# The MLPs of the last two token blocks as one 2x2 block product with seven products, and the sample tokens moved to block 1

## The chip, the core and the metric

The kernel runs on one core of a Trainium2 chip. The metric is device time in microseconds (us), median of three runs. The engines are named as in the profile: PE is TensorE (matmuls; PEld its weight loads), DVE is VectorE, ACT is ScalarE, POOL is GpSimd, SP is SyncE, which here only issues DMAs.

## The reference, cut to what matters

One decoder layer over 2048 prompt tokens and 32 sample tokens (8 sequences of 4), width 1024, MLP width 4096, all fp32:

```
mod = silu(c) @ ada_w + ada_b ;  sh1, sc1, g1, sh2, sc2, g2 = split(mod, 6)
h    = rmsnorm(x) * (1 + sc1) + sh1
proj = h @ w_in                       # columns for three token mixers
y    = concat(ssd(...), rwkv(...), s5(...))     # scans over the tokens, with states
x    = x + g1 * (y @ w_out)
h2   = rmsnorm(x) * (1 + sc2) + sh2
ff   = square(relu(h2 @ mlp_w1)) @ mlp_w2       # 1024 -> 4096 -> 1024
y_out = rmsnorm(x + g2 * ff) ;  the mixers' states are outputs too
```

## The kernel before

**Tiling.** Features lie on the 128 partitions, tokens on the free axis. The prompt is cut into four blocks of 512 tokens (`NB`, `BT`); the 32 sample tokens ride with block `SB` = 2, which is so 544 columns wide (`W`) and is multiplied as two pieces of 272. A PE product is done in `fp32r`, a rounded fp32, as three matmuls per 128x128 weight tile: high part by high part, high by low, low by high (`gemm`, `gemm2`). ACT rounds a tensor to its high part and DVE or POOL subtracts to get the low part, for weights (`wprep`, `wlow`, 512 columns at a time in a ring `wring` of four) and for activations. For blocks 0 and 1 the low part of a weight is split, 224 columns on DVE and 288 on POOL (`WS.POOL`); for blocks 2 and 3 all 512 columns are on DVE.

**Stages.** `in_proj` for blocks 0 to 3; then, block by block, `out_proj`, the last four output tiles of the block before (`w2_chunk` from `HOLD` = 4 on), `final_gen` of the block before (final norm and output) and `mlp`. `mlp` runs eight chunks: four tiles of `mlp_w1` (24 matmuls each) fill the hidden layer, eight tiles of `mlp_w2` (12 each) take it to the output, where DVE adds it to `xs` (`resid`). The MLP of one 512-token block has 1536 matmuls of 128x512. `norm2_gen` makes the second norm's output between `out_proj` and `mlp`.

**Order.** The program is written out by a planner in Python (`Plan`, `pump`): it keeps rough clocks of the engines, and between groups of four matmuls (`SLOT`) it lets waiting generators write their next instructions. The mixers of all blocks (`ssd_gen`, `rw_gen`, `rw_prep`, `rw_post`, `s5_gen`) are such generators: chains of small PE, DVE, ACT and POOL instructions that are interleaved with the large matmuls of `in_proj` and of the MLPs of blocks 0 and 1. `wait_for` and `until` stop the writing of large matmuls until a flag is set, and let only generators write meanwhile. `out_proj(b)` so waits for the mixers of block b alone (`mix_flags`). Buffers come from a few arenas (`Mem`), PSUM banks from two lists: three for large products, five for the rest. All DMAs are issued on SP's queue in program order. Every instruction is recorded by one helper, so a profile row's line is always L198 and groups differ by tiles and shapes: `arena` is fp32 memory, `arena_r` the rounded one, `bk` a PSUM bank.

## Time and profile before

| | us |
|---|---|
| median of 3 runs | 2868.09 (2866.37 to 2869.43) |
| span of the profiled execution | 2863.7 |
| PE busy | 2739.5 |
| DVE busy | 1967.3 |
| ACT busy | 1142.5 |
| POOL busy | 653.5 |

The span is the time between the first and the last instruction of one profiled execution; a run's time also holds what lies around it, here 4.4 us by the median. Stage borders used below are counted off along the program's order of large matmuls: `in_proj` 29 to 799, `out_proj` of block 0 to 870, MLP of block 0 to 1394, MLP of block 1 from 1469 to 1962, of block 2 from 2033 to 2417, of block 3 from 2477 to 2846.

### The profile page before, as it was taken

The numbers are of one execution on the slowest core, as the hardware profiler recorded it, in microseconds if no ns is written. First come the engines' busy times: TensorE is split into PE (matmuls) and PEld (weight loads), VectorE is DVE, ScalarE is ACT, GpSimd is POOL, SyncE is SP. The second block draws the span as 40 slices with busy tenths as digits, with TensorE's granted clock in tenths as the row PEclk, the third lists the DMA queues.
The fourth block names the chain that finished last, engine by engine and source line by source line (L and its number), as shares of the span: only waits on it lengthen the run. The fifth ranks groups of instructions, "written<-read, shape, count | busy, mean of one in ns | idle before, by whom it ended". The sixth has DMA issues, their size and how long they took to land.

```text
span 2863.7 us, 45369 instructions
## 1 busy us (share of the span) xinstructions
PE 2739.5 (96%) x16651; PEld 2265.7 (79%) x16651; DVE 1967.3 (69%) x4567; ACT 1142.5 (40%) x2153; POOL 653.5 (23%) x829
## 2 busy tenths in 40 slices
PE   7999889999999999999999999999999999999997
PEld 4677778877777777777777777778899999888886
DVE  6988996887997877666676778676653535643434
ACT  4354443454335432233443432334534344433342
POOL 1234432233442233322323343321000000000000
PEclk9999999999999999999999999999999999999999
DMA  8467656446553444433434364334222223232222
GB/s 284 155 213 252 201 163 198 164 155 215 170 191 115 144 125 155 146 115 97 159 129 135 118 188 142 120 118 151 96 89 89 89 89 133 82 126 96 99 93 74
DMA packets 302667, 406.26 MB, mean 142 GB/s; under 512 B 85604, under 2 KB 197348, under 8 KB 302444
## 3 DMA queue, kind: packets, MB, share of 16 engines
q1 hardware_dynamic: 302444, 403.36, 42.8%
q8 instruction: 131, 2.15, 0.3%
q14 instruction: 92, 0.75, 0.1%
HBM read 329.67 MB, written 73.62 MB: 141 GB/s over the span
## 4 chain that ended last, share of the span: by engine, by line
PE 62%; DVE 9%; issue 2%; ACT 1%; DMA 1%; POOL 0%; SPq 0%; DVEq 0%; POOLq 0%; ACTq 0%
PE bk L198 62%; DVE arena L198 7%; DVE arena_r L198 2%; ACT arena L198 1%; ACT arena_r L198 1%; DMA arena<-sph 0%; DMA arena<-spk 0%; POOL arena L198 0%; DMA arena<-in_w_out 0%; POOL arena_r L198 0%; DMA arena<-spl 0%; SPq L198 0%; DVEq L198 0%; DVEq L2724 0%; POOLq L198 0%
## 5 line engine op out<-in xcount | busy, mean ns | idle before, releaser
L198 PE MATMUL bk<-arena_r 128*128 128x512 f32 (+1 forms) x11344 | 2284.7, 358 | 61.7 <-DVE arena_r L198 41.5
L198 PEld LDWEIGHTS bk<-arena_r 128*128 128x128 f32 x11344 | 1843.9, 190 | 397.9 <-DVE arena_r L198 65.4
L198 DVE TENSOR_TENSOR arena_r<-arena,arena_r 128x224 fp32r<-128x224 f32 (+2 forms) x981 | 577.7, 610 | 416.9 <-ACT arena_r L198 410.6
L198 ACT ACTIVATE arena_r<-arena 128x512 fp32r<-128x512 f32 (+1 forms) x976 | 581.5, 627 | 468.4 <-PE bk L198 394.3
L198 POOL TENSOR_TENSOR arena_r<-arena,arena_r 128x288 fp32r<-128x288 f32 (+1 forms) x530 | 510.7, 976 | 1055.2 <-ACT arena_r L198 933.2
L198 ACT ACTIVATE arena<-bk 128x512 f32<-128x512 f32 (+8 forms) x619 | 271.9, 459 | 1008.5 <-PE bk L198 798.3
L198 PE MATMUL bk<-arena 128*128 128x128 f32 (+14 forms) x5139 | 540.3, 290 | 50.9 <-DVE arena L198 37.5
L198 PEld LDWEIGHTS bk<-arena 128*128 128x128 f32 (+6 forms) x5139 | 429.7, 152 | 179.7 <-issue 71.2
L198 DVE TENSOR_TENSOR arena<-arena 128x512 f32<-128x512 f32 (+16 forms) x1286 | 515.2, 411 | 51.1 <-ACT arena L198 16.6
L198 DVE SCALAR_TENSOR_TENSOR arena<-bk,arena 128x512 f32<-128x512 f32 (+1 forms) x368 | 235.4, 644 | 269.7 <-PE bk L198 264.0
L198 ACT ACTIVATE arena<-arena 128x512 f32<-128x512 f32 (+4 forms) x445 | 290.1, 664 | 208.1 <-DVE arena L198 189.7
L198 DVE SCALAR_TENSOR_TENSOR arena<-arena 128x512 f32<-128x512 f32 (+9 forms) x605 | 252.2, 430 | 26.6 <-ACT arena L198 6.7
L198 DVE TENSOR_TENSOR arena<-bk,arena 128x512 f32<-128x512 f32 (+4 forms) x277 | 101.2, 381 | 37.0 <-PE bk L198 31.4
L198 POOL TENSOR_TENSOR arena<-arena 128x512 f32<-128x512 f32 (+1 forms) x56 | 73.6, 1320 | 193.5 <-DVE arena L198 100.2
L198 DVE TENSOR_TENSOR arena<-arena,bk 128x512 f32<-128x512 f32 (+2 forms) x163 | 100.4, 627 | 15.3 <-PE bk L198 12.6
L198 DVE SCALAR_TENSOR_TENSOR arena<-arena,bk 64x64 f32<-64x64 f32 (+3 forms) x278 | 91.4, 355 | 27.4 <-PE bk L198 24.1
L198 DVE TENSOR_SCALAR arena<-arena 128x4 f32<-128x4 f32 (+14 forms) x359 | 95.8, 289 | 13.6 <-ACT arena L198 7.8
L198 POOL COPY arena<-arena 128x3 f32<-128x3 f32 (+6 forms) x222 | 70.0, 327 | 47.3 <-ACT arena L198 29.9
L198 ACT ACTIVATE arena<-bk,arena 128x512 f32<-128x512 f32 (+4 forms) x112 | 57.0, 535 | 17.8 <-PE bk L198 16.6
L198 DVE COPY arena<-bk 64x256 f32<-64x256 f32 (+5 forms) x85 | 43.6, 513 | 4.1 <-PE bk L198 2.6
L198 DVE TENSOR_TENSOR_SCAN arena<-arena 128x256 f32<-128x256 f32 (+2 forms) x40 | 36.1, 902 | 1.3
L198 DVE TENSOR_REDUCE arena<-arena 128x4 f32<-128x256 f32 (+1 forms) x34 | 14.0, 412 | 6.7 <-ACT arena L198 6.4
(14 smaller groups left out, 46.3 us busy)
## 6 DMA issues: line engine op xcount, KB each, us to landing
arena<-in_w SPq DMA_DIRECT2D x256, 512.0 KB
arena<-in_w_in SPq DMA_DIRECT2D x88, 512.0 KB
arena<-in_ada_w SPq DMA_DIRECT2D x24, 1024.0 KB
arena<-in_x SPq DMA_DIRECT2D x64, 256.0 KB
arena<-spk SPq DMA_DIRECT2D x32, 512.0 KB
arena<-in_w_out SPq DMA_DIRECT2D x32, 512.0 KB
spk<-arena SPq DMA_DIRECT2D x40, 256.0 KB
spl<-arena SPq DMA_DIRECT2D x33, 256.0 KB
```

The costliest lines, as they stand in the source:

```text
L198: r = fn(*a, **k)
```

## The change

**Pairing.** Only blocks 0 and 1 run `mlp` as before (`NPLAIN` = 2). Blocks 2 and 3 go through a new function `paired`. It takes the two blocks as the two columns of a 2x2 matrix of blocks, and splits the weights' inner and outer dimension in two, so that h2 @ W is a product of 2x2 block matrices. Seven products of sums and differences give what eight plain ones give (the Strassen-Winograd form). For `mlp_w1` the right-hand sums (B11, T2, B21, T3, T1, T4, B22) are made once by `right_gen`. For `mlp_w2` the hidden layer's seven units are made by `hid_gen`, stored to DRAM (`sp_hid`), read back, and split into high and low parts by `hid_load`. The sums of weight blocks (S1 to S4) are made on POOL as the program runs (`Sums`), and all low parts of weights in `paired` past the two `project` calls are made on POOL too.

**What `paired` writes, in order:** the seven state outputs (they stood at the program's end before); `project(0)`, the output projection of block 2; the last four output tiles of block 1's MLP; `project(1)`, for block 3; three early products with B11 and B21 (`NPRE` = 3), while `right_gen` makes the sums; 16 rounds for `mlp_w1` (seven products of 12 matmuls; five in the first three); 16 half rounds for `mlp_w2` (14 products of 6 matmuls); then `final_gen` for both blocks.

**Around it.** `SB` is 1. `mlp` of block 1 waits in its sixth chunk until the mixers of blocks 2 and 3 are all done, since their arena (`arena_b`) is handed over to `paired` as rounded memory (`arena_t`). The RWKV mixer's sample part is written with fewer, wider instructions. The scratch memory for dynamic DMA is made smaller.

```diff
-SB = 2
+SB = 1
+NPLAIN = 2
+NPRE = 3
@@ mlp
+            if b + 1 == NPLAIN and c == 5:
+                for q in range(NPLAIN, NB):
+                    for fl in mix_flags(q) + [("rwb", q)]:
+                        until(fl)
+                A1[:] = [M1]
...
@@ wlow
+                P.tensor_tensor(sm.shape(lo.r), wsrc.pop(i), sm.shape(hi.f), ALU.subtract)
+                sm.drop(wops[i][2])
@@ class Sums
+        def get(self, name):
+            if name == "S2":
+                self.sum("S1", blk("21"), blk("22"), ALU.add)
+                self.sum("S2", self.shape(t["S1"].f), blk("11"), ALU.subtract)
+            elif name == "S3":
+                self.sum("S3", blk("11"), blk("21"), ALU.subtract)
+            elif name == "S4":
+                self.sum("S4", blk("12"), self.shape(t["S2"].f), ALU.subtract)
...
@@ right_gen, for k in (4, 0, 5, 1, 6, 2, 7, 3)
+                scaled(b_[k], bk, k)
+                if k >= 4:
+                    yield 0
+                    continue
+                yield
+                tt(a[k].f, b_[k].f, a[k].f, ALU.subtract)
+                tt(b_[k].f, b_[k + 4].f, b_[k].f, ALU.subtract)
+                yield from put("B22", b_[k + 4].f, True)
+                tt(b_[k + 4].f, b_[k + 4].f, a[k].f, ALU.subtract)
+                tt(a[k + 4].f, a[k + 4].f, b_[k + 4].f, ALU.subtract)
+                yield from put("T2", b_[k + 4].f, True)
+                yield from put("T3", b_[k].f)
...
@@ for p in range(16)
+            product(bkb, wop(), 0, Units("T2"), True)
+            u2 = mal(n)
+            tt(u2.f, u1.f, bkb, ALU.add)
...
+            product(bkc, wop(), 0, Units("T3"), True)
+            tt(u3.f, u2.f, bkc, ALU.add)
+            product(bkd, wop(), 0, Units("T1"), True)
+            tt(c["22"].f, u3.f, bkd, ALU.add)
+            product(bkc, wop(), 0, Units("T4"), False)
+            tt(c["21"].f, u2.f, bkc, ALU.add)
+            product(bkd, wop(), 0, Units("B22"), False)
+            tt(c["12"].f, u2.f, bkd, ALU.add)
...
@@ for c in range(8), half in range(2), nm in UNITS, e, mp in enumerate(mps)
+                        product(bk, w, 256 * e, un, fresh)
+                        if nm == "11" and c == 0:
+                            act(z.f, bk)
+                        elif nm in ("11", "S2"):
+                            tt(z.f, z.f, bk, ALU.add)
+                        elif nm == "12":
+                            add(x11, g0)
...
```

**Where instructions move.** On PE, late in block 1's MLP. Before, groups of large products (`arena_r 128x512`) and of the mixers' small ones take turns:

```order
L198 MATMUL bk_66<-arena_r 128x512 x12
L198 MATMUL bk_68<-arena 128x128 x2
L198 MATMUL bk_70<-arena 64x64 x4
L198 MATMUL bk_69<-arena 32x2x64 x8
L198 MATMUL bk_67<-arena_r 128x512 x12
L198 MATMUL bk_65<-arena_r 128x512 x4
L198 MATMUL bk_72<-arena 32x2x64 x8
L198 MATMUL bk_65<-arena_r 128x512 x16
```

After, from the last large product that stands ahead of the wait in the sixth chunk (`arena_r 128x272`, since the block now carries the sample tokens) on, 385 small ones of the mixers follow without a large one between them (twelve of them read `arena_r` too, in the SSD mixer), of which these are the first:

```order
L201 MATMUL bk_70<-arena_r 128x272 x24
L201 MATMUL bk_72<-arena,arena_b 128x128 x4
L201 MATMUL bk_74<-arena_b,arena 128x512 x2
L201 MATMUL bk_72<-arena_b 64x64 x8
L201 MATMUL bk_73<-arena,arena_b 128x128 x4
L201 MATMUL bk_75<-arena,arena_b 128x1 x4
L201 MATMUL bk_72<-arena_b 32x2x64 x8
L201 MATMUL bk_75<-arena 128x128
L201 MATMUL bk_73<-arena_b 32x2x64 x8
L201 MATMUL bk_76<-arena_b,arena 128x512 x2
```

The mixers' remainder has moved out of the shade of the large products into one piece of its own; on DVE 257 instructions stand in the same piece.

On DVE, between `project(1)` and the first rounds of `mlp_w1`; `bk_74` is the broadcast norm factor of block 3. There `right_gen` stands in four groups of eight instructions, before the first eviction of a `mlp_w1` round that uses one of its sums (the `bk_71` row):

```order
L201 TENSOR_TENSOR arena<-arena,bk_74 128x512 x2
L201 TENSOR_TENSOR arena<-arena 128x512 x4
L201 TENSOR_TENSOR arena_r<-arena,arena_r 128x512 x2
L201 TENSOR_TENSOR arena<-arena,bk_74 128x512 x2
L201 TENSOR_TENSOR arena<-arena 128x512 x4
L201 TENSOR_TENSOR arena_r<-arena,arena_r 128x512
L201 TENSOR_TENSOR arena<-arena,bk_71 128x512
L201 TENSOR_TENSOR arena_r<-arena,arena_r 128x512
```

These are the last two groups; before, `norm2_gen` stood there with two instructions for each of eight feature tiles.

On POOL, in one half round for `mlp_w2`, where before POOL had nothing to do (its last instruction stood in block 1's stretch):

```order
L201 TENSOR_TENSOR arena<-arena 128x512
L201 TENSOR_TENSOR arena_r<-arena,arena_r 128x512 x3
L201 TENSOR_TENSOR arena<-arena 128x512
L201 TENSOR_TENSOR arena_r<-arena,arena_r 128x512 x2
L201 TENSOR_TENSOR arena<-arena 128x512 x2
L201 TENSOR_TENSOR arena_r<-arena,arena_r 128x512 x2
```

Eleven instructions of 512 columns for each round: seven low parts (`arena_r`) and four sums (`arena`).

## Rows read from the trace of the kernel before

**Rows 1.** The page: span, PE and GB/s in 40 slices

```profile
span 2863.7 us, 45369 instructions
PE 2739.5 (96%) x16651; PEld 2265.7 (79%) x16651; DVE 1967.3 (69%) x4567; ACT 1142.5 (40%) x2153; POOL 653.5 (23%) x829
GB/s 284 155 213 252 201 163 198 164 155 215 170 191 115 144 125 155 146 115 97 159 129 135 118 188 142 120 118 151 96 89 89 89 89 133 82 126 96 99 93 74
```

**Rows 2.** Busy time by stretch: MLPs of blocks 0, 1, 2, 3; the tail

```profile
core 0: us, PE busy (x) PEld busy (x) DVE busy (x) ACT busy (x) POOL busy (x), PEclk, DMA share, GB/s
870.00:1394.00 524.00, 518.15 (x3161) 402.98 (x3160) 373.41 (x888) 204.35 (x388) 162.00 (x181) 1.00 0.42 133
1469.00:1962.00 493.00, 475.69 (x2639) 376.41 (x2640) 364.17 (x812) 190.63 (x347) 165.47 (x180) 0.99 0.43 140
2033.00:2417.00 384.00, 379.45 (x2999) 378.38 (x3000) 194.27 (x455) 156.86 (x311) 0.00 (x0) 0.99 0.28 97
2477.00:2846.00 369.00, 363.04 (x1569) 294.33 (x1567) 167.48 (x278) 144.90 (x244) 0.00 (x0) 0.99 0.27 92
2846.00:2863.70 17.70, 4.02 (x24) 3.65 (x24) 7.02 (x19) 0.07 (x1) 0.00 (x0) 0.60 0.41 150
```

**Rows 3.** Busy time by stretch, inside the MLPs of blocks 3 and 2

```profile
2720.00:2820.00 100.00, 100.00 (x435) 81.26 (x434) 39.58 (x61) 38.96 (x66) 0.00 (x0) 1.00 0.27 94
2200.00:2300.00 100.00, 100.00 (x801) 100.00 (x800) 46.60 (x107) 38.28 (x77) 0.00 (x0) 1.00 0.25 85
```

**Rows 4.** Busy time by stretch: the last wait of block 0's `out_proj`

```profile
853.60:870.50 16.90, 15.20 (x139) 13.38 (x137) 13.86 (x32) 8.27 (x16) 2.98 (x4) 0.80 0.23 71
```

**Rows 5.** Groups by form (count | busy us, mean ns | idle), 2520 to 2820, POOL idle

```profile
L198 DVE TENSOR_TENSOR arena_r<-arena,arena_r 128x512 fp32r<-128x512 f32 x135 | 88.1, 684 | 108.5 <-ACT arena_r L198 108.5
L198 ACT ACTIVATE arena_r<-arena 128x512 fp32r<-128x512 f32 x135 | 78.8, 625 | 103.3 <-PE bk L198 102.5
L198 DVE SCALAR_TENSOR_TENSOR arena<-bk,arena 128x512 f32<-128x512 f32 x56 | 42.0, 750 | 66.9 <-PE bk L198 66.9
```

**Rows 6.** Groups by form, 870 to 1394, POOL at work

```profile
L198 DVE SCALAR_TENSOR_TENSOR arena<-bk,arena 128x512 f32<-128x512 f32 x59 | 44.1, 748 | 44.7 <-PE bk L198 44.1
L198 DVE TENSOR_TENSOR arena_r<-arena,arena_r 128x512 fp32r<-128x512 f32 x45 | 38.2, 852 | 13.9 <-ACT arena_r L198 13.6
...
L198 DVE TENSOR_TENSOR arena<-arena 128x1024 f32<-128x1024 f32 x5 | 7.1, 1418 | 0.2
...
L198 POOL TENSOR_TENSOR arena_r<-arena,arena_r 128x512 fp32r<-128x512 f32 x20 | 23.1, 1174 | 5.8 <-PE bk L198 5.8
```

**Rows 7.** Groups by form, the whole run

```profile
L198 DVE SCALAR_TENSOR_TENSOR arena<-arena 128x512 f32<-128x512 f32 x176 | 146.6, 840 | 9.0 <-ACT arena L198 4.5 <-PE bk L198 0.9 <-POOL arena L198 0.8
...
L198 POOL TENSOR_TENSOR arena<-arena 128x504 f32<-128x504 f32 x16 | 26.1, 1637 | 53.9 <-DVE arena L198 53.3 <-PE bk L198 0.7
```

**Rows 8.** Timeline of DVE (start us, us), the last RWKV chunk

```profile
1956.60 0.58 DVE L198 TENSOR_TENSOR arena<-bk,arena 64x128 f32<-64x128 f32 x2
...
1972.23 1.17 DVE L198 SCALAR_TENSOR_TENSOR arena<-arena,bk 64x64 f32<-64x64 f32 x4 [4.17 <-PE bk L198]
...
1982.85 0.88 DVE L198 TENSOR_TENSOR arena<-arena 128x256 f32<-128x256 f32 x2
```

**Rows 9.** Timeline, start of block 3's MLP

```profile
2482.31 12.17 PE L198 MATMUL bk<-arena_r 128*128 128x512 f32 x41 [4.34 <-ACT arena_r L198]
...
2484.22 0.81 ACT L198 ACTIVATE arena<-arena 128x512 f32<-128x512 f32 x1 [1.44 <-DVE arena L198]
```

**Rows 10.** Timeline, the end

```profile
2844.65 0.75 DVE L198 SCALAR_TENSOR_TENSOR arena<-bk,arena 128x512 f32<-128x512 f32 x1 [1.40 <-PE bk L198]
...
2852.15 5.35 DVE L198 SCALAR_TENSOR_TENSOR arena<-arena,bk 128x512 f32<-128x512 f32 x8 [2.17 <-PE bk L198]
...
2857.92 0.45 SPq L198 DMA_DIRECT2D out_p_conv<-arena  x1
...
2860.80 0.43 SPq L198 DMA_DIRECT2D out_p_rwkv<-arena  x1
```

More of the change, by code (lines that the diff above doesn't have):

```diff
@@ new lines, in tail_ops @@
+    def tail_ops(e, block, shape, names):
+        sm = Sums(e, block, shape)
+        for name in names:
+            wops.append([e + 1, sm, name])
+    if len(wseq) % 2:
+        wseq.append((d["w_out"][0], "pad"))
+    flat = lambda t: t
+    for p_ in range(NPRE):
+        e = len(wseq)
+        wseq.append((d["w1"][2 * p_], "m1"))
+        sm = Sums(e, one_block(e), flat)
+        wops.append([e, sm, "11"])
+        wops.append([e, sm, "12"])
+    if len(wseq) % 2:
+        wseq.append((d["w1"][0], "pad"))
@@ L2532, in layer_kernel @@
     for b in range(NB):
-        rest = in_proj(b, nxt[b])
-        next(rest, None)
+        in_proj(b, nxt[b])
     until(("ada", 11))
     last = None
-    for b in range(NB):
+    for b in range(NPLAIN):
         WS.POOL = 0 if b > 1 else 288
```

514 lines of the change are left out of this document (437 added, 77 removed).

## The prediction

> **What bounds the kernel now.** I read the page first, then busy time by stretch, then the groups by form inside stretches with and without POOL, last the timeline where blocks change. PE is busy 96% of the span, so the span is PE's time plus its waits, 2863.7 - 2739.5 = 124 us [rows 1]. By stretch the picture differs. In the MLPs of blocks 2 and 3 PE is nearly always busy while DVE is at half its time and POOL is idle; there a removed matmul is time won. In the MLPs of blocks 0 and 1 the mixers run in the matmuls' shade, DVE is at 71 and 74%, POOL at a third [rows 2]. Inside block 3's MLP 435 matmuls of 128x512 take 100 us, so one costs 0.230 us, at a granted clock of 1.00; a 272-column one costs 0.125 us (801 in 100 us) [rows 3].
>
> **Part 1, the seven products.** The MLP of two blocks has 2 x 1536 = 3072 matmuls of 128x512; an eighth of them, 384, goes. In the order 6832 such matmuls are 6448 after, and the 4512 of 272 columns stay. 384 x 0.230 = **-88.3 us**, all on the path in the stretch where PE is the only busy engine.
>
> **Part 2, the wait in block 1's MLP.** The mixers' rest, hidden before, stands alone: 385 small PE instructions without a large product. The nearest row is the wait at the end of block 0's `out_proj`, where 73 such instructions take 16.9 us with PE busy 15.2 and DVE 13.9 [rows 4]. By PE's count the piece takes 385/73 x 16.9 = 89 us, of which 80 us is PE work that is due in any order: a loss of 9. By DVE's count (257 against 32 records) it takes 257/32 x 13.9 = 112 us: a loss of 32. What stands against both is the chain: of the last RWKV chunk, state and post-processing alone went from 1956.6 to 1983.7 [rows 8], beside large products. I count from the order some four chunks left; one after the other, with the two state steps (15.6 us up to 1972.2) and as much again for the preparation, and 10 us behind the last, they take 4 x 31 + 10 = 134 us, a loss of 54. Below I take 5: the 9 of PE's count rests on one row, and a gain is excluded, since the PE work itself is due in any order. I take **+20 us**, between the two counts, since the same mixture of engines made rows 4. Queued behind the waiting products on PE is the whole rest of the program.
>
> **Part 3, the sums for `mlp_w1`.** `right_gen` starts when block 3's norm factor is there. From the last residual to the first use of such a factor it took 7.5 us [rows 10]; here some of the early products stand in between on PE, about 4 us more. Then come one ACT step of 0.81 [rows 9], four DVE steps of about 0.7, an ACT rounding of 0.63 [rows 5] and a POOL low part of 1.17 [rows 6]: the first T2 unit at about 17 us. Each further group holds eight DVE instructions, 8 x 0.684 = 5.5 us [rows 5], 6 at POOL's side; the fourth unit is there at 17 + 3 x 5.5 = 33.5 to 35 us. PE's cover is three early rounds, 72 x 0.230 = 16.6 us, and 4 us of small matmuls; T2's product would end at 20.6 + 2.8 = 23.4 and ends at about 35: 12 us, and 2 more for what follows such a wait (41 matmuls in 12.2 us instead of 9.4 [rows 9]). **+14 us**, bounds 8 and 20.
>
> **Part 4, the start of `mlp_w2`.** Twelve x tiles of 256 KB are issued on SP at its first product, ahead of 1 MB of weights and of the hidden unit that the fifth product needs: 4.5 MB at the highest rate that the page shows, 284 GB/s [rows 1], is 16 us. The product comes after 4 x 2.76 = 11 us and needs its operand 2.5 us before for the split. **+6 us**, bounds 0 (the queue is ahead) and 12.
>
> **Part 5, the steady rounds.** One round is 84 matmuls, 19.3 us. POOL has 11 instructions, 11 x 1.17 = 12.9 us [rows 6]. DVE has, for `mlp_w1`, five evictions (0.68 to 0.75), three of 0.84 [rows 7] and four of 0.85: 9.5 us; for `mlp_w2`, 14 evictions of about 0.73 and 3.5 splits of 1.42 [rows 6]: 15.2 us. ACT: eleven or so of 0.63 to 0.8, 8 us. DMA: 2.8 MB a round, 145 GB/s, which many slices of the page exceed [rows 1]. All lie below 19.3, so PE should bound; but stretches with DVE at three quarters and POOL at a third have PE waiting 1.1 and 3.5% [rows 2]. On 602 us that is 6 to 21; the stretch had hardly any before. I take **+8 us**, bounds 0 (PE was at 100% there, so no gain) and 21. The rows show what DVE and POOL do to each other: a DVE subtraction with both inputs in SBUF takes 0.684 us with POOL idle [rows 5] and 0.852 beside POOL, an instruction that reads PSUM 0.750 and 0.748 [rows 5, 6]. The Trainium skill, "SBUF — State Buffer", section "Who interferes with whom", says that a DVE instruction with two SBUF inputs and a GpSimd instruction that reads SBUF exclude each other for the whole instruction, the second waiting until the first ends; the rows agree in kind. By that rule the two engines' shares add up in `paired`, and that is the first rival below.
>
> **Part 6, the end.** Two blocks instead of one run `final_gen` last: eight more instructions (5.35 us for eight [rows 10]) and the second norm's small steps, about 1 us, less the seven state outputs, which go from the end to the start of `paired`: 7 x 0.47 = 3.3 us of issue from 2857.9 to 2861.2 [rows 10]. **+3 us**, bounds 0 and 6. In their new place the outputs stand on SP ahead of block 2's x tiles, 3.3 us, which are first needed after 24 matmuls, 5.5 us: covered.
>
> **Part 7, at nothing.** The sample tokens move with all their matmuls; nothing is added. The RWKV sample part needs some 30 DVE instructions fewer beside the matmuls of `in_proj`, where PE bounds too, and the changed arenas reorder the early stretch: 0, with 10 either way. 60 weight loads go, 112 stores and 56 loads of the hidden units come; SP issues one in some 0.47 us, and a store that waits for DVE holds the next weights for a round at most, which the ring of four raw buffers covers.
>
> **The sum.** -88.3 + 20 + 14 + 6 + 8 + 3 = -37 us on 2863.7: a span of 2826.4. The median of the runs lies 4.4 above the span, so the time is **2831 us**.
>
> **Rivals.** (a) *DVE and POOL exclude each other and bound `paired`.* For `mlp_w2` the low parts and sums read weight blocks with strides. The nearest strided POOL row is 1.637 us for 504 columns [rows 7]. With that, 11 x 1.637 + 3.5 x 1.42 = 23.0 us a half round against 19.3, +58 us over 16; in `mlp_w1`, 11 x 1.25 + 3 x 0.84 + 4 x 0.85 = 19.7, +6. 2831 - 8 + 64 = **2887**, slower than before. It decides from a POOL mean of (19.3 - 5.0)/11 = 1.30 us. For it: the rows of contention; against it: contiguous ones are at 1.17, runs of 128 are longer than the 63 of that row, and four of seven low parts are contiguous. (b) *The mixers' chains run one after the other* at the wait, loss 54 instead of 20: **2865**, no change. For it: rows 8; against: rows 4, with DVE busy 82% of such a wait. (c) *Nearly all waits are hidden*: 5 + 8 + 0 + 0 + 3, **2796**. For it: PE waits only 1% beside block 0's mixers; against it: T2's fourth unit has no cover. (d) That the change doesn't do what it says: the order shows the 384 fewer, so I give it nothing.
>
> **How the numbers follow.** The forecast has 0.65, (a) 0.12, (b) 0.08, (c) 0.15. A measurement of this kernel can tell about 0.2%, 6 us, from no change. Forecast and (c) are faster; (b) is half faster, half the same; of (a) 0.10 is slower and 0.02 the same. Faster 0.84, same 0.06, slower 0.10. All low bounds together give -75 - 10 and 2783, all high ones 2903, neither likely at once; the range reaches to (c) below and towards (a) above, leaving out about one in ten on each side: 2795 to 2880.
>
> **What would show it.** In the profile after: 6448 matmuls of 128x512 at 0.230; a stretch of 90 to 110 us late in block 1's MLP with PE at 75 to 90% and DVE above it; a PE wait of about 12 us before the first products with T2, released by POOL or DVE; PE at 97% or more in the steady rounds, with POOL near 1.2 us an instruction. Wrong would be the forecast if the steady rounds take over 20 us each, or if the wait for the mixers leaves PE idle for half of it.

## The result, and the profile after

The changed kernel takes 2937.5 us (median; 2932.9 to 2945.8) against 2868.8 for the kernel before on the same chip: 1.0242 times as long, interval 1.0221 to 1.0263. The forecast was 2831, with 2795 to 2880 as its range. The profiled execution spans 2931.1 us, 67.4 more than before; the forecast span was 2826.4. So 105 us have to be found.

The page of the changed kernel, span, PE's row and the granted clock in 40 slices, answers to [rows 1]:

```profile
span 2931.1 us, 45771 instructions
...
PE 2703.2 (92%) x16267; PEld 2238.9 (76%) x16267; DVE 2120.2 (72%) x4588; ACT 1100.8 (38%) x2049; POOL 1212.6 (41%) x1220
...
PEclk9999999999999999999999999978998999999998
```

PE's idle time went from 2863.7 - 2739.5 = 124 us to 2931.1 - 2703.2 = 228, so the waits grew by 104. PE's busy time fell by 36, where the 384 matmuls that are gone are worth 88, so 52 are missing. The groups of PE's large forms say where most of them are (count | busy us, mean ns of one | idle); first before, then after:

```profile
L198 PE MATMUL bk<-arena_r 128*128 128x512 f32 x6832 | 1693.3, 401 | 46.7 <-DVE arena_r L198 34.3 <-ACT arena_r L198 10.9 <-POOL arena_r L198 0.7
L198 PE MATMUL bk<-arena_r 128*128 128x272 f32 x4512 | 593.2, 292 | 15.0 <-ACT arena_r L198 7.7 <-DVE arena_r L198 7.2
```

```profile
L201 PE MATMUL bk<-arena_r 128*128 128x512 f32 x4864 | 1230.0, 403 | 58.2 <-DVE arena_r L201 27.2 <-ACT arena_r L201 24.8 <-DVE arena L201 2.2
L201 PE MATMUL bk<-arena_r 128*128 128x272 f32 x4512 | 614.6, 294 | 46.4 <-DVE arena_r L201 22.5 <-ACT arena_r L201 13.1 <-DVE arena L201 8.9
...
L201 PE MATMUL bk<-arena_t,arena_r 128*128 128x512 f32 x1584 | 399.3, 402 | 26.6 <-DVE arena_t L201 12.0 <-ACT arena_t L201 7.7 <-ACT arena L201 3.7
```

4864 + 1584 = 6448 matmuls of 128x512, as the order said. But they took 1230.0 + 399.3 = 1629.3 us, where 1693.3 - 88.3 = 1605.0 were left to do: 24 us more. The 4512 of 272 columns took 21 us more, and the mixers' small ones the rest. There is more waiting, and PE is slower around the waits.

Busy time by stretch of the changed kernel, to be read beside [rows 2] and [rows 3]. In order: MLP of block 1 up to the wait, and the wait; the three early rounds and the first full round of `mlp_w1`; steady rounds of `mlp_w1` (3 to 15); the first half round of `mlp_w2`; later half rounds; from the last large matmul to the end:

```profile
core 0: us, PE busy (x) PEld busy (x) DVE busy (x) ACT busy (x) POOL busy (x), PEclk, DMA share, GB/s
1466.80:1865.60 398.80, 380.62 (x3110) 355.33 (x3110) 319.40 (x810) 147.84 (x305) 120.35 (x130) 0.98 0.40 125
1865.60:1998.30 132.70, 92.62 (x692) 68.81 (x693) 85.42 (x257) 30.27 (x67) 15.13 (x16) 0.75 0.27 85
2219.30:2287.60 68.30, 40.44 (x157) 29.73 (x156) 36.60 (x48) 27.06 (x46) 40.84 (x30) 0.78 0.14 50
2306.00:2550.00 244.00, 242.12 (x1042) 196.51 (x1042) 122.49 (x153) 70.22 (x123) 187.68 (x137) 0.99 0.43 157
2571.00:2609.00 38.00, 26.00 (x84) 18.97 (x83) 24.86 (x25) 13.82 (x18) 18.82 (x13) 0.82 0.78 296
2630.00:2860.00 230.00, 228.97 (x993) 185.74 (x992) 188.35 (x210) 90.42 (x124) 201.91 (x132) 1.00 0.41 142
2905.60:2931.10 25.50, 9.52 (x49) 8.84 (x48) 19.41 (x47) 2.05 (x4) 0.00 (x0) 0.60 0.43 165
```

The steady stretches are as forecast: 1042 matmuls in 244 us and 993 in 230 are 0.234 and 0.232 us each, with PE at 99%. Three stretches stand out by PE's share and clock: the wait in block 1's MLP (70% busy, clock 0.75), the start of `mlp_w1` (59%, 0.78) and the start of `mlp_w2` (68%, 0.82).

**The wait.** The timeline of PE on either side of it (start us, us):

```profile
1858.65 6.87 PE L201 MATMUL bk<-arena_r 128*128 128x272 f32 x52
...
1998.37 11.84 PE L201 MATMUL bk<-arena_r 128*128 128x272 f32 x77
```

In between stand 132.7 us with small PE work only. No engine is full in them: PE 70%, DVE 64%, ACT 23%, POOL 11%. DVE's timeline shows the last state steps of four RWKV chunks, 31, 17 and 28 us apart:

```profile
1896.15 1.22 DVE L201 SCALAR_TENSOR_TENSOR arena<-arena,bk 64x64 f32<-64x64 f32 x4 [0.80 <-PE bk L201]
...
1926.67 1.16 DVE L201 SCALAR_TENSOR_TENSOR arena<-arena,bk 64x64 f32<-64x64 f32 x4 [0.18 <-PE bk L201]
...
1943.46 1.22 DVE L201 SCALAR_TENSOR_TENSOR arena<-arena,bk 64x64 f32<-64x64 f32 x4
...
1971.78 1.22 DVE L201 SCALAR_TENSOR_TENSOR arena<-arena,bk 64x64 f32<-64x64 f32 x4 [1.32 <-PE bk L201]
```

**The start of `mlp_w1`.** PE's timeline in the first full round, where T2's product takes one unit after the other:

```profile
2244.51 0.50 PE L201 MATMUL bk<-arena_t,arena_r 128*128 128x512 f32 x1 [0.71 <-POOL arena_r L201]
2252.72 0.79 PE L201 MATMUL bk<-arena_t,arena_r 128*128 128x512 f32 x1 [7.70 <-ACT arena_t L201]
...
2262.31 0.80 PE L201 MATMUL bk<-arena_r 128*128 128x512 f32 x1 [7.03 <-ACT arena_r L201]
...
2271.91 0.80 PE L201 MATMUL bk<-arena_r 128*128 128x512 f32 x1 [7.02 <-ACT arena_r L201]
```

The units come 9.6 us apart; the prediction had 5.5 to 6. DVE's timeline shows what fills one such step: eight instructions, 8.1 us, and two short waits for ACT, 1.5 us:

```profile
2256.17 1.27 DVE L201 TENSOR_TENSOR arena<-arena,bk 128x512 f32<-128x512 f32 x2
2258.43 3.89 DVE L201 TENSOR_TENSOR arena<-arena 128x512 f32<-128x512 f32 x4 [0.99 <-ACT arena L201]
2262.81 3.02 DVE L201 TENSOR_TENSOR arena_r<-arena,arena_r 128x512 fp32r<-128x512 f32 x2 [0.49 <-ACT arena_r L201]
2265.76 1.27 DVE L201 TENSOR_TENSOR arena<-arena,bk 128x512 f32<-128x512 f32 x2
```

### The profile page after: what moved, and what is told of

Same layout as the page of the kernel before. It is cut to its first block, busy times and chain, and to the rows that moved or that the text cites. A ratio compares the mean times of both kernels' runs of the same rounds, so it can differ in the third digit from the quotient of the medians.

```text
span 2931.1 us, 45771 instructions
## 1 busy us (share of the span) xinstructions
PE 2703.2 (92%) x16267; PEld 2238.9 (76%) x16267; DVE 2120.2 (72%) x4588; ACT 1100.8 (38%) x2049; POOL 1212.6 (41%) x1220
## 4 chain that ended last, share of the span: by engine, by line
PE 55%; DVE 13%; issue 3%; ACT 2%; DMA 2%; SPq 1%; POOL 0%; DVEq 0%; ACTq 0%; POOLq 0%
PE bk L201 55%; DVE arena_b L201 6%; DVE arena L201 5%; DVE arena_r L201 2%; ACT arena_b L201 1%; SPq L201 1%; ACT arena_r L201 1%; DVE arena_t L201 0%; DMA arena_b<-in_st_ssd 0%; ACT arena L201 0%; DMA arena_b<-spx 0%; DMA arena<-in_x 0%; DMA arena<-spr 0%; DMA spl<-arena_b 0%; POOL arena_r L201 0%
## 5 line engine op out<-in xcount | busy, mean ns | idle before, releaser
L201 PE MATMUL bk<-arena_r 128*128 128x512 f32 (+1 forms) x9376 | 1841.2, 351 | 104.7 <-DVE arena_r L201 49.7
L201 PEld LDWEIGHTS bk<-arena_r 128*128 128x128 f32 x9376 | 1495.2, 191 | 360.6 <-DVE arena_r L201 64.8
L201 POOL TENSOR_TENSOR arena_r<-arena,arena_r 128x288 fp32r<-128x288 f32 (+2 forms) x795 | 880.7, 1121 | 1461.8 <-ACT arena_r L201 1282.6
L201 ACT ACTIVATE arena_b<-bk 128x512 f32<-128x512 f32 (+9 forms) x453 | 192.9, 448 | 754.1 <-PE bk L201 513.6
L201 DVE TENSOR_TENSOR arena_r<-arena,arena_r 128x224 fp32r<-128x224 f32 (+2 forms) x552 | 294.8, 542 | 204.4 <-ACT arena_r L201 200.3
L201 PE MATMUL bk<-arena_t,arena_r 128*128 128x512 f32 x1584 | 399.3, 402 | 26.6 <-DVE arena_t L201 12.0
L201 PEld LDWEIGHTS bk<-arena_t,arena_r 128*128 128x128 f32 x1584 | 302.8, 192 | 102.9 <-DVE arena_t L201 14.5
L201 DVE TENSOR_TENSOR arena_b<-arena_b 128x256 f32<-128x256 f32 (+17 forms) x531 | 267.6, 512 | 22.5 <-ACT arena_b L201 8.1
L201 DVE SCALAR_TENSOR_TENSOR arena<-bk,arena 128x512 f32<-128x512 f32 (+2 forms) x330 | 200.9, 627 | 104.4 <-PE bk L201 103.2
L201 PE MATMUL bk<-arena_b 32*32 32x128 f32 (+9 forms) x2352 | 215.8, 278 | 17.7 <-DVE arena_b L201 6.0
```

The lines of the kernel that those rows point to most:

```text
L201: r = fn(*a, **k)
```

## The experiments

Each run stands beside runs of the kernel before on its chip. The last column is the ratio's distance from 1, times 2869; the intervals reach 4 to 7 us to either side, so a difference between two runs is uncertain by 6 to 9 us.

| run | what | us | ratio (interval) | against before |
|---|---|---|---|---|
| | the change | 2937.5 | 1.0242 (1.0221 to 1.0263) | +69 |
| e1 | before, sample tokens in block 1 | 2897.3 | 1.0084 (1.0065 to 1.0103) | +24 |
| e2 | e1 and the wait | 2980.8 | 1.0373 (1.0351 to 1.0396) | +107 |
| e13 | e1 and the wait for block 2 alone | 2894.7 | 1.0087 (1.0064 to 1.0109) | +25 |
| e5 | e1, smaller request for room | 2899.4 | 1.0110 (1.0091 to 1.0130) | +32 |
| e9 | before, no MLP for sample tokens | 2840.1 | 0.9905 (0.9887 to 0.9924) | -27 |
| e10 | e1, no MLP for sample tokens | 2849.8 | 0.9938 (0.9921 to 0.9955) | -18 |
| e3 | change, wait late | 2891.8 | 1.0071 (1.0050 to 1.0092) | +20 |
| e4 | change, six early rounds | 2932.9 | 1.0217 (1.0199 to 1.0234) | +62 |
| e6 | e3, sums in passes | 2892.8 | 1.0085 (1.0068 to 1.0102) | +24 |
| e7 | e3, mixers earlier | 2929.2 | 1.0206 (1.0181 to 1.0232) | +59 |
| e8 | e7 with e6's passes and more | 2930.0 | 1.0215 (1.0198 to 1.0233) | +62 |
| e11 | e3, four generators for the sums | 2887.6 | 1.0074 (1.0059 to 1.0090) | +21 |
| e12 | e11, x tiles earlier | 2890.2 | 1.0075 (1.0052 to 1.0098) | +22 |
| e14 | e11, low parts on DVE | 2878.8 | 1.0030 (1.0015 to 1.0045) | +9 |
| e15 | e14, five early rounds | 2884.7 | 1.0052 (1.0032 to 1.0071) | +15 |
| e16 | e14, hidden units first | 2880.1 | 1.0040 (1.0027 to 1.0053) | +11 |
| e17 | e16, swap behind block 2's `out_proj` | 2886.4 | 1.0064 (1.0045 to 1.0083) | +18 |

### The change taken apart: the move, the wait, the seven products

e1, one line of the kernel before:

```diff
-SB = 2
+SB = 1
```

> The kernel before with one edit: the sample tokens go with block 1 instead of block 2. No wait in block 1's MLP, no arena swap, eight products. In the changed kernel 104 us are missing against the forecast. Theory W (the wait): the price is that of the wait in block 1's MLP, the move alone costs nothing where mixers of blocks 2 and 3 may run on until out_proj of those blocks: 2869, within 8 us either way. Theory M (the move): the sample part of the RWKV stage holds up the mixers of the blocks behind it and lengthens the stages up to block 1's MLP, as the longer out_proj stages of the changed kernel suggest (93 + 72 us instead of 72 + 60): 2895 to 2915 here. Theory S (the seven-product section is what is dear): 2869 as well, so this run tells M from the other two.

e2, the same and, in `mlp`:

```diff
         for c in range(7):
+            if b == 1 and c == 5:
+                for q in range(2, NB):
+                    for fl in mix_flags(q) + [("rwb", q)]:
+                        until(fl)
```

> The kernel before with two edits: sample tokens with block 1, and the wait for all mixers of blocks 2 and 3 in block 1's MLP at chunk 5. Nothing else of the change. Theory W: the mixers left at that place (some 300 small PE instructions, the RWKV chunks one behind the other) take 130 to 150 us nearly alone on PE, of which 80 to 95 is PE work that is due anyway: 45 to 65 us above the run with the sample tokens alone, so 2915 to 2930. Theory M: most is in the move, the wait adds the 20 us of the forecast: 20 above the run with the move alone. Theory S: both small, 2870 to 2890.

Measured: +24 for the move (theory W had none, theory M 25 to 45), and 107 - 24 = +83 for the wait, more than any theory had. What is left of the change, the seven products with all that goes with them, is 69 - 107 = -38. The traces bear it out. In e2 as in the change the mixers are done at the end of block 1's MLP; from there to the end, first e2, then the change:

```profile
2111.80:2970.30 858.50, 832.84 (x3680) 679.11 (x3678) 400.99 (x679) 332.24 (x559) 0.00 (x0) 0.98 0.31 102
```

```profile
2110.30:2931.10 820.80, 759.00 (x3296) 613.46 (x3294) 550.98 (x726) 290.94 (x455) 561.52 (x398) 0.96 0.42 150
```

That is 37.7 us less, with 384 matmuls fewer. The section is a gain, as forecast (without the wait and with the move at nothing the forecast was -57). The wait and the move make it a loss. In e2 the stretch of the wait, by the same view, is longer than in the change and emptier:

```profile
1828.80:1999.60 170.80, 103.26 (x755) 78.13 (x755) 107.59 (x310) 34.45 (x76) 21.43 (x21) 0.70 0.25 72
```

e13, e2 without block 3 in the wait:

```diff
-                        until(fl)
+                        if q == 2:
+                            until(fl)
```

> The kernel before with the sample tokens in block 1 (2897) and a wait at chunk 5 of block 1's MLP for the mixers of block 2 alone, where the run with the wait for blocks 2 and 3 took 2981. Theory: what the wait costs is block 3's mixers, which without a pair of blocks are due only at block 3's out_proj, some 490 us later; block 2's are due 180 us later anyway and nearly done. In the order the largest piece without a large product is 20 small PE instructions here and 174 there. 2897 to 2907. If any wait for all of a block's mixers at that place costs (the mixers stand in the order of their ranks, a chunk of block 2 as late as one of block 3): 2920 or more.

Measured: +25, the same as without any wait (e1, +24). The price is that of block 3's mixers alone: taken singly, block 3's `out_proj` needs them only some 490 us later, and a pair needs its arena now.

e3, the changed kernel with the wait at the other end of block 1's MLP:

```diff
@@ mlp, loop over the chunks
-            if b + 1 == NPLAIN and c == 5:
-                for q in range(NPLAIN, NB):
...
@@ mlp, behind the last w2_chunk
+        if b + 1 == NPLAIN:
+            for q in range(NPLAIN, NB):
...
```

> The changed kernel with the wait moved from chunk 5 of block 1's MLP to behind its last product (the accumulator of the squares then lies in M1, as the residuals do). Some 107 us of products of that MLP then run beside the mixers' rest; in the order the largest piece without a large product falls from 150 small PE instructions to 60. Theory W: 35 to 50 us below the changed kernel, 2890 to 2900. Theory S: the section of seven products bears the loss, so less than 15 us: 2922 to 2937.

Measured: 69 - 20 = 49 us less, theory W. (The expectation counts pieces between any two products of `arena_r`, the SSD mixer's among them; so its largest piece is 150 where the whole wait has 385.) The last stretch of block 1's MLP still shows a wait, 50 us of PE work in 63 at clock 0.88:

```profile
2000.00:2063.40 63.40, 49.96 (x394) 44.18 (x394) 49.86 (x139) 25.76 (x55) 12.88 (x14) 0.88 0.29 92
```

### Why the move costs 24 us

e5, `rw_gen` of the block with the sample tokens asks for less room:

```diff
-        spawn(after([("pre", b)] + prev, rw_gen(b), C_RW + (2600 if b == SB else 0), R_RW(b), ("rwb", b)), R_RW(b))
+        spawn(after([("pre", b)] + prev, rw_gen(b), C_RW, R_RW(b), ("rwb", b)), R_RW(b))
```

> The kernel before with the sample tokens in block 1, as in the run with the move alone (2897, 24 above before), and with one number changed: rw_gen of the block with the sample tokens asks for 7200 columns of the mixers' room at its start instead of 9800. Theory A (admission): the larger request stands at the head of the queue until 9800 columns are free, every mixer behind it starts later, and block 0's MLP hides less of them; in the order block 0's MLP holds 603 small PE instructions with the move alone, 888 before, 708 here. Then about a third of the 24 us and what was pushed into block 2's out_proj (147 small PE instructions there, none here) come back: 2875 to 2886. Theory B (the sample part itself is dear where it now stands, in DVE and PE work): unchanged, 2892 to 2902.

Measured: +32 against +24, the intervals overlap: theory A falls. The mixers moved forward as the order said, and nothing came back: block 0's MLP took 510 us instead of 481, and from the last tiles of block 0's `mlp_w2`, behind block 1's `out_proj`, to the start of block 1's MLP 48 us passed instead of 18, with PE idle for 26 of them.

e9 and e10 leave out the MLP of the sample tokens, once in block 2 and once in block 1:

```diff
-        w1_tail(b, gemm(ap, b == SB, drop), hid)
+        w1_tail(b, gemm(ap, False, drop), hid)
...
@@ w2_chunk, and so in mlp
-        hasS = b == SB
+        hasS = False
```

> The kernel before with the MLP of the 32 sample tokens left out (their columns of the residual go on to the end as they are); block 2's MLP is then 1536 products of 512 columns instead of 3072 of 272. By the rows this takes 1536 x (0.250 - 0.230) = 31 us off a stage where PE is the only busy engine: 2838, within 6. It is the base for the next run.

> The same with the sample tokens in block 1 (the move alone, 24 us above before), their MLP left out. Theory D: the move costs because the sample tokens' part of the MLP, its 272-column products, evictions and splits, now stands in the MLP that DVE shares with the mixers, while in block 2's it had DVE half free; without that part the move is free, so 0 to 8 us above the run before this one, 2838 to 2846. Theory M: the price lies in the sample part of the mixers and of in_proj and out_proj, which comes earlier than before and pushes other mixers back: 24 above, 2862.

Measured: -27 and -18, a price of 9 or 10 for the move without that MLP where it was 24 with it. So the larger part, some 14 us (give or take 9), lies in the MLP of the sample tokens, as theory D has it: 272-column products, with twice the evictions, in an MLP where DVE also has the mixers (74% busy there before, 51% in block 2's [rows 2]). That DVE's load is what makes them dearer there was not tested by itself, and what makes the other 10 was not found.

### The rest of the wait

e7, e3 with e5's edit and

```diff
-    MARGIN2, LAG4 = 1100, 2300
+    MARGIN2, LAG4 = 600, 3500
```

> The changed kernel with the wait late (2892), the sample tokens' rw_gen at 7200 columns, and the planner's two numbers for the mixers beside the MLPs at margin 600 and lag 3500 instead of 1100 and 2300, so that mixers are written earlier in the program. In the order block 0's MLP then holds 786 small PE instructions instead of 629, and the largest piece without a large product in block 1's MLP falls from 60 to 20. Theory A: what is left of the wait and of the move goes, 20 to 30 us: 2862 to 2872. If the order on DVE then makes the large products wait elsewhere in block 0's MLP: 2885 to 2900.

Measured: 39 us slower than e3. Busy time of the MLPs of blocks 0 and 1, first e7, then e3:

```profile
892.97:1443.00 550.03, 521.55 (x2926) 409.10 (x2927) 404.62 (x932) 198.77 (x367) 160.68 (x191) 0.97 0.43 133
...
1553.70:2101.10 547.40, 519.75 (x4287) 487.90 (x4287) 397.04 (x1024) 200.90 (x418) 144.23 (x161) 0.98 0.37 118
```

```profile
885.80:1370.50 484.70, 475.60 (x2684) 375.36 (x2684) 334.42 (x740) 182.62 (x335) 159.96 (x181) 0.99 0.43 136
...
1464.20:2063.40 599.20, 563.46 (x4666) 522.79 (x4667) 464.60 (x1201) 221.17 (x459) 165.39 (x180) 0.97 0.39 122
```

242 more PE records in block 0's MLP cost 65 us there and give back 52 in block 1's. PE's idle time in block 0's MLP goes from 9 to 28 us, and its clock from 0.99 to 0.97. (Block 0's MLP also starts 7 us later, and the stretch between the MLPs takes 17 more.) Mixers that are written earlier are no longer ready when PE comes to them; that this is their chains of DVE and ACT steps was not tested.

e17, e16 (below) with the wait and the swap moved behind `project(0)`:

```diff
@@ mlp, behind the last w2_chunk
-        if b + 1 == NPLAIN:
...
@@ paired
-        spawn(y2_gen(), 0.3)
         project(0, ys, left_gen)
+        for q in blocks:
...
+        wait_for(lambda: MB1.used == 0, "swap")
...
+        spawn(y2_gen(), 0.01)
```

> The run before this one with the wait for block 3's mixers, and the swap of the arena with it, moved once more, from the end of block 1's MLP to behind block 2's out_proj; y2_gen, which splits block 3's y for its out_proj, then starts behind the swap instead of ahead of block 2's out_proj, at the front of the order. With the wait late the last 63 us of block 1's MLP hold PE work of 44 us; that loss of 19 goes behind 44 us of block 2's out_proj. y2_gen's eight loads and splits (46 us in the changed kernel, beside other work) then have only the 15 us of the last chunk of block 1's mlp_w2 as cover: at 2.5 us each 20 us, a loss of 5 to 8. Sum: 11 to 14 less than the run before. If y2_gen takes as long as now: 15 us slower.

Measured: no gain, +18 against +11. Block 1's MLP, block 2's `out_proj`, the last chunk of block 1's `mlp_w2` and block 3's `out_proj` took 570.9, 57.0, 29.6 and 57.4 us; in e16 the same four took 602.6, 46.7, 14.8 and 52.3. The 32 us won in the first come back in the other three: 10, 15 and 5. Ahead of a pair stands a path through block 3's last mixers, their y and `out_proj`, and moving the swap only moves where PE waits for it.

### The start of `mlp_w1`

e4, `NPRE = 6` instead of 3 in the change:

> The changed kernel with six instead of three early rounds (products with block 2's own units alone) ahead of the first product with T2: 72 more matmuls, 16.6 us, stand where PE waited for the sums of right_gen. In the trace that piece (early rounds and first full round) takes 68 us where its 132 matmuls need 30. Forecast from the wait there: 16 us less, 2921. If the sums are late because DVE, ACT and POOL are slow and not because of when they begin, each early round is worth its full 5.5 us: 2921 too. If PE's wait only moves (the units B11 and B21 wait for the same engines), 2932 to 2940.

e6, e3 with `right_gen` in passes:

```diff
+                yield from put("T2", b_[k + 4].f)
...
+            for k in range(4):
+                yield from put("T3", b_[k].f)
...
```

> The changed kernel with the wait late (2892) and right_gen in passes: all four B22 and T2 first, then T3, then T1, then T4, instead of all five operands of a unit at a time; T2's low part goes to DVE instead of POOL. In the changed kernel PE got T2's units 9.6 us apart, three such gaps in the first full round. Per T2 unit the passes leave two scalings, four subtractions and a low part on DVE instead of eight to ten instructions in all: some 5.5 to 6.5 us apart. If DVE's count sets the spacing: 10 us less, 2882. If the chain of ACT and POOL low parts in between sets it (each step waits for another engine), 2888 to 2892. If later operands then come late instead: 2892 or more.

e11, e3 with `right_gen` as four generators:

```diff
-            for k in (4, 0, 5, 1, 6, 2, 7, 3):
+            def one(k):
...
+            for k in range(4):
+                spawn(one(k), 0.001 * k)
```

> The changed kernel with the wait late (2892) and right_gen as four generators, one for each pair of units, instead of one that takes the pairs one after the other; the same instructions. In the trace T2's units came 9.6 us apart while DVE was at 61%, ACT at 41% and POOL at 66% in that stretch, and passes in another order left the time where it was. Theory chain: each step waits for another engine and the one generator lets nothing else be written in between; with four of them PE loses 10 to 15 us less in the first full round, 2877 to 2882. Theory engines: the units' own DVE, ACT and POOL time sets the end, 2888 to 2894. If the first unit comes later because all four share the engines: 2892 or more.

Measured: -7 against the change for e4 (16 expected; the intervals overlap), and +24 and +21 against e3's +20 for e6 and e11, no difference. In e11 T2's units no longer come 9.6 us apart, but the early rounds wait instead: early rounds and first full round together take 59.1 us against 67.0 in e3. The whole does not show these 8 us, nor can it rule them out. So neither another order of the sums, nor four generators, nor more cover takes the loss away by itself. DVE's groups by form in that stretch of the change point to another cause; the number behind the busy time is the mean of one in ns:

```profile
L201 DVE TENSOR_TENSOR arena<-arena 128x512 f32<-128x512 f32 x16 | 16.0, 999 | 6.0 <-ACT arena L201 4.0 <-POOL arena_t L201 1.5
L201 DVE TENSOR_TENSOR arena_r<-arena,arena_r 128x512 fp32r<-128x512 f32 x5 | 7.7, 1554 | 1.0 <-ACT arena_r L201 1.0
L201 DVE TENSOR_TENSOR arena<-arena,bk 128x512 f32<-128x512 f32 x9 | 5.8, 679 | 2.6 <-PE bk L201 2.6
```

and POOL's there:

```profile
L201 POOL TENSOR_TENSOR arena_r<-arena,arena_r 128x512 fp32r<-128x512 f32 x12 | 17.4, 1459 | 13.3 <-ACT arena_r L201 13.3
```

A subtraction with both inputs in SBUF takes 1.00 or 1.55 us instead of 0.684 [rows 5], POOL's 1.46 instead of 1.17 [rows 6], and a DVE instruction that reads PSUM 0.679. (e6 moved T2's four low parts from POOL to DVE, but left eight others there.) e14 takes POOL out of `right_gen`, on e11:

```diff
-                yield from put("T2", k, b_[k + 4].f, True)
+                yield from put("T2", k, b_[k + 4].f)
```

(and so for B22 and T1; `True` puts the low part on POOL).

> The run with four generators for right_gen (2888) with the twelve low parts that it gives to POOL on DVE. In its trace DVE's subtractions with both inputs in SBUF took 1.20 and 1.57 us there instead of the 0.68 they take with POOL idle, and those that read PSUM 0.68. Theory exclusion: the two engines' SBUF work adds up, 24 x 0.68 on DVE and 12 x 1.17 plus the weights' low parts on POOL; twelve at 0.68 instead of 1.17 take 6 us off: 2880 to 2884. If the engines work side by side: DVE's own work grows by 8 us, 2888 to 2896.

Measured: +9 against e11's +21, 12 us less. That is theory exclusion: the 6 us expected lie at the edge of what the intervals leave (6 to 19). DVE has twelve instructions more, and those with two inputs in SBUF are still shorter, means of 0.84 and 1.22 us, in e14:

```profile
L201 DVE TENSOR_TENSOR arena_r<-arena,arena_r 128x512 fp32r<-128x512 f32 x12 | 13.9, 1217 | 0.0
L201 DVE TENSOR_TENSOR arena<-arena 128x512 f32<-128x512 f32 x16 | 13.2, 841 | 0.9 <-ACT arena L201 0.5
```

than in e11:

```profile
L201 DVE TENSOR_TENSOR arena<-arena 128x512 f32<-128x512 f32 x16 | 18.6, 1195 | 3.2 <-POOL arena_t L201 2.4 <-ACT arena L201 0.5
L201 DVE TENSOR_TENSOR arena_r<-arena,arena_r 128x512 fp32r<-128x512 f32 x6 | 9.2, 1570 | 0.0
```

The stretch takes 54.7 us against 59.1. The spans of the two profiled executions differ by 6 us, so 4.4 of 6 lie here; whether the rest of the 12 is more than scatter is open. The weights' low parts are still on POOL.

e15, e14 with `NPRE = 5`:

> The run before with five early rounds instead of three: 48 matmuls, 11 us, in front of the first product with T2. If the early rounds run while right_gen works: 8 to 11 us below the run before, 2872 to 2876. In the run with six of them on the changed kernel only 5 of 16 us came back, with POOL at 63% and DVE at 52% beside them; if the early rounds' own steps (two low parts of weights on POOL, one eviction and one rounding on ACT each) push right_gen back: 0 to 4 us below.

Measured: +15 against +9, no gain; the spans of the two profiled executions are equal, 2878.4 and 2878.6. In e15's trace the first full round runs without a wait, 60 matmuls in 13.8 us, so T2's units are in time. But the early rounds in front of it wait, 10.9 us in all, each time for an ACT instruction that empties a PSUM bank. With more cover the loss moves from T2's product to the early rounds.

### The start of `mlp_w2`

e12, e11 with the first four x tiles loaded from round 12 on:

```diff
             for mp in range(4):
+                if mp:
+                    yield from need("rounds")
...
+            if p == 12:
+                spawn(x_load(), 0.3)
```

e8, e7 with e6's passes, a fourth early round, and half of the x tiles behind the first chunk's hidden units:

```diff
             for mp in range(4):
+                while mp > 1 and len(HU[0]) < 7:
+                    yield
```

e16, e14 with hidden units first, and `final_gen` of each block started inside the last chunk:

```diff
-                spawn(hid_load(), 0.25)
+                spawn(hid_load(), 0.02)
...
+                    spawn(late(0), 0.01)
+                    spawn(late(1), 0.01)
```

> The run before with the first four x tiles and their sum tile (1 MB of the 4 MB that x_load brings at the start of mlp_w2) loaded from round 12 of mlp_w1 on instead of behind round 15. The first half round of mlp_w2 lost 19 us, in a stretch where DMA moved 296 GB/s. If the transfers set that loss: 1 of the 11 MB of that stretch less, 3 to 4 us below the run before. If the split of the hidden units on ACT and DVE sets it, or their memory, which is free only when mlp_w1's units are spent: no difference within 3 us. If the tiles taken early leave too little memory for rounds 12 to 15: slower by 5 or more.

> All together on the changed kernel: wait late, mixers early (both edits of the run before), right_gen in passes, four early rounds instead of three, and x_load stops behind its first eight tiles until the seven hidden units of the first chunk are split, so that these stand ahead of the other eight x tiles on SP. If the parts add up: 2867 - 10 (sums) - 2 (a fourth early round) - 5 (of the 19 us that the first half round of mlp_w2 lost) = 2850, 0.7% below the kernel before. If the mixers' part gives nothing: 2875.

> The run with right_gen as four generators and its low parts on DVE (2879), with two edits. hid_load goes ahead of hid_gen in the planner's order (rank 0.02 instead of 0.25), so that the splits of mlp_w2's first hidden units don't stand on DVE behind round 15's differences, which only the last chunk needs; and final_gen of each block starts as soon as its own norm is there, not behind the loop. If DVE's order sets the 19 us that the first half round of mlp_w2 loses: 8 to 12 us less there, 2868 to 2871. If the transfers set it (16 MB between 2558 and 2598 in the changed kernel, at about 400 GB/s): the half round stays at 38 to 40 us. The end: 2 us less if block 2's outputs run beside the last product, else nothing, since DVE is busy 87% of the last half round and the end.

The first half round took 38.2 us in the change and 39.9 in e11, 40.0 in e12, 43.6 in e8, 39.5 in e14, 34.8 in e16; 84 matmuls are 19.3. A quarter of the x tiles earlier (e12) or half of them later (e8) gave nothing, so it does not hang on where these 1 or 2 MB stand. Ahead on DVE the hidden units gave 5 us, as the first theory of e16 has it, but that is a quarter of the loss, and the whole of e16 shows no gain (+11 against +9). What remains fits the transfers: GB/s of the change in 40 slices of 2550 to 2612 us stands near 400 from 2562 to 2598:

```profile
GB/s 11 0 0 0 166 342 254 285 407 404 366 386 404 410 403 407 418 408 391 407 379 363 375 406 378 382 406 411 412 418 398 284 37 0 0 0 0 0 0 0
```

That was not tested by taking the transfers away.

As for e8 as a whole, it inherits e7's loss: +62 beside e7's +59. No version that does the whole work beat the kernel before; the nearest is e14, +9.

## Why the prediction was wrong, step by step

| part | forecast | found | from |
|---|---|---|---|
| 1, seven products | -88 | -88 | 6448 matmuls, 0.232 to 0.234 us in steady rounds |
| 2, the wait | +20 | +53 | 132.7 us less the 80 of PE work due; e3 takes 49 of it away |
| 3, the sums | +14 | +34 | 68.3 us less 132 x 0.230 and 4 |
| 4, start of `mlp_w2` | +6 | +19 | 38.2 less 19.3 us |
| 5, steady rounds | +8 | +7 | 556 us for 2388 matmuls |
| 6, the end | +3 | +11 | 49.3 us less 19.3, against 19.1 before |
| 7, the sample tokens | 0 | +24 | e1 |

The found parts add up to +60 of the +67 us of the span. That they come so near is partly luck. Parts 3 to 5 are taken against PE's bare time, and eight products do not run at that either: in e2 the MLPs of blocks 2 and 3 take 717.7 us for 3024 matmuls, 22 more than 0.230 each. The forecast made the same slip, which brought it nearer to the result. The section's two stretches in e2 and the change are the cleaner measure: -38, where parts 1 and 3 to 6 as found add up to -17. By that the wait, with what else the change does ahead of the pair, costs 67 + 38 - 24 = 81 us and not 53; e2 gives 83.

Some of the difference lies at the front, which part 7 put at 0 "with 10 either way". From the start to block 0's MLP, first before, then the change, then e1:

```profile
0.00:870.50 870.50, 799.62 (x5077) 636.71 (x5077) 735.45 (x1818) 381.71 (x755) 299.58 (x433) 0.97 0.60 194
```

```profile
0.00:886.00 886.00, 802.47 (x5037) 638.85 (x5037) 687.09 (x1728) 379.30 (x759) 294.33 (x427) 0.96 0.56 184
```

```profile
0.00:845.40 845.40, 783.94 (x4963) 620.10 (x4963) 669.54 (x1670) 376.92 (x755) 290.51 (x419) 0.97 0.59 192
```

PE idles 71 us there before, 84 in the change and 61 in e1, which has the move alone. Whether the new arenas or the rewritten RWKV sample part make it was not tested.

**Part 2** failed where a value was chosen between two counts. Three stood there: 89 us for the piece by PE's count, 112 by DVE's, 134 by the chain of four RWKV chunks. The piece took 132.7. The forecast lay between the first two because [rows 4] were taken for the same mixture of engines. But in [rows 4] DVE was busy 82% of the time, and here 64%: it was not the same mixture, and the chunks came one behind the other, as [rows 8] had shown it. Rival (b) described it; its chance of 0.08 was the error. That the count of 134 comes within 2 us is partly luck: it had four steps of 31 us and 10 behind the last, and the trace has steps of 31, 17 and 28 and 25 behind the last. That the chain sets the piece is read from the trace (no engine full, the state steps 17 to 31 us apart), and no run took the chain away. That the wait as such is the price, and that block 3's mixers are, is shown by e2, e3 and e13.

**Part 7** was put at nothing because "the sample tokens move with all their matmuls". It did not ask beside what they stand afterwards. The rows were there: DVE at 51% in block 2's MLP and at 74% in block 1's [rows 2]. e1 gives 24 us, e9 and e10 some 14 of them for the MLP's part. (e1 has the RWKV sample part as it was; in the changed kernel the move was not taken by itself.)

**Part 3** had the right wait and the wrong spacing: eight DVE instructions of 0.684 for a unit, with POOL beside them for nothing. In the trace the eight take 8.1 us, and 1.5 of waiting for ACT come on top. T2's first unit came at 22.5 us behind the last residual instead of 17, partly because its low part stood on POOL behind sums and a low part of weights, and the fourth at 54 instead of 35. The prediction used the exclusion of DVE and POOL for a rival on the steady rounds, but not here, where DVE and POOL work on the same sums. The Trainium skill, "SBUF — State Buffer", section "Who interferes with whom", says that a DVE instruction with two SBUF inputs contends with a GpSimd instruction that reads SBUF, and that one with at most one SBUF input outside the two-port modes does not; the trace agrees: 1.00 and 1.55 us instead of 0.684, and 0.679 for the ones that read PSUM.

**Rival (a)** put that exclusion into the steady rounds, to decide from a POOL mean of 1.30 us. The mean was above that, first from 2300 to 2560 us (steady rounds of `mlp_w1`), then from 2650 to 2850 (half rounds):

```profile
L201 POOL TENSOR_TENSOR arena_r<-arena,arena_r 128x512 fp32r<-128x512 f32 x93 | 128.8, 1403 | 56.8 <-ACT arena_r L201 56.8
```

```profile
L201 POOL TENSOR_TENSOR arena_r<-arena,arena_r 128x512 fp32r<-128x512 f32 x74 | 115.4, 1576 | 25.2 <-ACT arena_r L201 25.2
```

Yet PE stayed at 99%. A mean of 1.58 already holds POOL's waits for DVE: in the timeline an undisturbed POOL instruction takes 1.3 us, one that meets a DVE split up to 2.3. The rival's sum set its 1.637 as POOL's own time and added DVE's to it. By undisturbed times the two engines need 11 x 1.30 + 3.5 x 1.22 = 18.6 us, just below a half round's 19.3. So the exclusion is there, but it does not bound, by a small margin, and part 5 was right: 1212 matmuls in 283.4 us and 1176 in 272.6 are 4.6 and 2.1 us over 0.230 each.

**Part 4** took 4.5 MB at 284 GB/s, the highest slice of the page. It left out what goes over the same queue there: 14 stores of the last round's hidden units (256 KB each), and 13 loads of hidden units and 4 of weights (512 KB each), with the x tiles some 16 MB. They run from 2557 to 2598, and a first half round without loss would end at 2571 + 19 = 2590. The mechanism may be right and the size was wrong, by a count that left most of the queue out; that transfers set all of it was not shown.

**Part 6** counted the outputs and not what DVE does before them. The timeline of the end, PE's last large matmuls, the last sum of squares, and the outputs on DVE:

```profile
2899.85 5.76 PE L201 MATMUL bk<-arena_t,arena_r 128*128 128x512 f32 x24
...
2909.17 2.31 DVE L201 TENSOR_TENSOR arena<-arena 128x512 f32<-128x512 f32 x3
...
2917.06 10.62 DVE L201 SCALAR_TENSOR_TENSOR arena<-arena,bk 128x512 f32<-128x512 f32 x16
```

The 16 outputs take 10.62 us, 5.3 more than the eight of [rows 10], as forecast. But behind PE's end at 2905.6 DVE needs 5.9 us more for the last evictions, the sums of z and the squares. Before it was 1.4: there the last eviction ended at 2845.4 [rows 10], and PE began the norm at 2846. And the last half round takes 23.8 us instead of 19.3.

**The clock** stands in no part of its own. PE's products ran at down to half speed behind the longer waits (the last section), so such a wait cost more than its idle time: 24 us idle made 30.6 in the first full round (44.4 us instead of 13.8), 12 made 19 in the first half round of `mlp_w2`. Part 3 had 2 us for that.

## What to carry to other kernels

When a change has two blocks of work start together, find what the second one needs, and price its whole remaining path by its chain too: here, where no engine was full, the longest count came out and not one in the middle. Moved work can cost by what it stands beside afterwards, even if not one instruction is added. Moving a wait later helps as long as other work can run in front of it (e3, 49 us), and stops helping where the next consumer needs the same result (e17). Before sums are shared out between DVE and POOL, count the instructions with two inputs in SBUF on both as one queue, at the times that they take undisturbed.

## What the runs showed of the hardware

**DVE and POOL.** With POOL reading SBUF, a 128x512 DVE subtraction of two SBUF operands took 0.84 to 1.57 us in the mean instead of 0.684, and POOL's 1.40 to 1.58 instead of 1.17; a DVE instruction with one PSUM operand stayed at 0.68. Putting twelve low parts from POOL on DVE gained 12 us (6 to 19 by the intervals), though DVE's own count grew.

**PE behind a wait.** In the first half round of `mlp_w2` PE waited and then took 5.49 us for 12 matmuls that take 2.76 in the steady rounds:

```profile
2584.43 5.49 PE L201 MATMUL bk<-arena_t,arena_r 128*128 128x512 f32 x12 [5.50 <-DVE arena_t L201]
```

That is 0.457 us for one, the rate at 1.2 GHz, where 0.230 is that at 2.4; the granted clock of the stretch is 0.82.

**Transfers.** At the start of `mlp_w2` the one queue that SP feeds moved 363 to 418 GB/s for 36 us (slices of 1.6 us), loads and stores together, well above the 284 of the page's slices of 72 us.
